# Second norm of a hybrid RWKV-7 / neighbourhood-attention layer: the third token tile finished in two halves, and two low weight halves made by adding DMAs

## The chip, the cores and the metric

The kernel runs on one core of a Trainium2 chip. TensorE (PE) multiplies, VectorE (DVE), ScalarE (ACT) and GpSimd (POOL) do the elementwise work, and SyncE (SP) issues most DMAs. The metric is the device time of one execution in microseconds (us); smaller is better. Before the change three runs gave a median of 1182.05 us (1181.28 to 1182.42).

## The reference, cut to what matters

One layer is applied to 128 context tokens and 512 latent tokens, with D = 1024 features. The change lies in its last third: the second RMS norm and the feed-forward part.

```python
x = x + g1 * (merged @ p["w_out"])
h2 = _rmsnorm(x, p["norm2_g"]) * (1.0 + sc2) + sh2
x = x + g2 * ((jax.nn.silu(h2 @ p["ffn_w1"]) * (h2 @ p["ffn_w3"])) @ p["ffn_w2"])
```

The hidden width of the feed-forward part is 2816, which is 22 tiles of 128 columns. All values are float32.

## The kernel before, in words

**Products.** Every float32 operand x is carried as two rounded tiles, a high half (x cast to fp32r) and a low half (x minus its high half). A product is the sum of three matmuls: high times high, high weight times low activation, low weight times high activation. `mm4` (L1797 to L1806) issues them in that order for four blocks of 128 features, so a group of 12 matmuls reads the weight's low half for the first time at its third matmul. `split` (L188 to L190) makes the two halves of an activation: an ACT cast and a DVE (or POOL) subtraction.

**Tokens.** The 640 tokens are five tiles of 128 (index i, where 0 to 3 are latent, 4 is context). For the feed-forward part they are regrouped into two halves of 320 tokens, n = 0 and n = 1, and the features into two halves q = 0 and q = 1; `hq[q, n]` holds the normed values and `B2[q, n]` their high and low tiles (named b in the trace). Tile 2 is cut in the middle: its first 64 tokens end the half n = 0 and its last 64 begin the half n = 1 (`cuts`, L1744).

**The second norm.** The last matmuls of the output projection (L288, tiles acc and m) are walked by `beside`, a loop that counts them. At given counts, listed in the string `n2`, it issues steps of the norm into the queues of the engines. Per tile i: A adds the projection into x (DVE L1683, L1684), S sums squares (ACT L1721), R takes the reciprocal root (DVE L247, POOL L248), X scales (DVE L1727), T and U transpose the two feature halves on PE (L1734) and apply scale and shift from PSUM (`n_out`: ACT L1740 for two blocks, DVE L1742 for the other two), and H and J split the two feature halves (`n_split`, L189 and L190). W loads and splits a feed-forward weight tile (L167, L177, L179). Steps issued at one count stand in the engines' queues in that order, and each engine works its queue strictly in order.

**After the projection.** The counting loop goes on through the first two hidden tiles (`conv_gen`, PE L1805, tile f), computed as plain products: 24 matmuls for each of two weights, for n = 0 of hidden tiles 0 and 1, then for n = 1. Beside them stand the rest of the norm (tiles 3 and 4), the four Strassen sums of the activations (D, DVE L1764) and their splits (E, tile t), and at count 230 the steps `Y0 Y2 K1 ... K8`: Y is the SiLU and product of a finished hidden tile (`conv_out`, L1823 on), K are the preparations of the first Strassen pair.

**Strassen pairs.** Hidden tiles 2 to 21 are computed by `pair`, one after the other: seven products of 12 matmuls instead of eight. The weights of a pair are g and u, two loaded tiles of 128x1024 (wst), and sums of their halves (ws, L1860, s1 to s4: s3 on POOL, the others on DVE). `preps` gives four weights, a (g itself), b (sums s3 and s1), c and d. Each is split by `w_hl`: the high half is an ACT cast (L1846, whi), the low half a DVE subtraction (L1849, wlo). For the first pair (hidden tile `FA` = 2) K1 to K8 run this in the order "s3 s1 s2 s4 ha la hb lb" (`w0`); for the later pairs the steps are spread over the products of the pair before (`wt`). The first product reads a, the second b, the third a again, and it adds into the sum of the first, which ACT has copied out before (L1886, tile p).

**Buffers.** The tile of g lives in a pool with one buffer, so the load of the next pair's g (SP, L167) waits until the last reader of this pair's g is done.

**The adding DMA elsewhere.** `wcast` (L171 to L180) has a second way to make a low half, used 26 times earlier in the program (between 252 and 601 us): ACT writes the negated rounded value into the low tile (L175), and a DMA issued by POOL adds the unrounded source onto it (L176).

Of the kernel before, what the change touches and what calls it, by code (L numbers as in the profile page):

```python
# [7 lines left out]
F32 = mybir.dt.float32  # L8
F32R = mybir.dt.float32r
AF = mybir.ActivationFunctionType  # L10
ALU = mybir.AluOpType
# [3 lines left out]
P = 128  # L15
# [7 lines left out]
XB, WAB, FA = 4, 8, 2  # L23
# [31 lines left out]
        "2 0 6 6 6 4 4 5 2 0 5 1 1 0 0"),  # L55
    qp=((0, 0, 7, 6, 7), (2, 5, 4, 4, 3, 2, 5, 3, 1)), ada=2, pa=1, pd=0,
    lw=(0, 0, 0, 0, 0, 2, 2, 2, 2, 2, 2, 2, 2, 2, 2, 2),
    n2=("48:A0S0 60:A1S1R0X0 72:A2S2R1X1 74:R2T0 76:U0X2H0J0 86:T1U1H1J1 89:W1 92:W0 100:T2U2H2J2 108:A3S3 "
     "120:A4S4R3X3R4X4W2W3 160:T3U3H3J3 180:T4U4H4J4 200:D1D3D2D4 210:E2E3E1 218:K0E4 "
     "230:Y0Y2K1K2K3K4K5K6K7K8 266:Y1"),  # L60
    te="dddddddd", pf=2, se="pddd", oe="d", w0="s3 s1 s2 s4 ha la hb lb",
# [40 lines left out]
def V(ap, dims, off=0):  # L102

    return bass.AP(ap.tensor, ap.offset + off, [list(ap.ap[0])] + [list(d) for d in dims])
# [3 lines left out]
def body(ctx: ExitStack, tc: tile.TileContext, xs, xp, cols, consts, w_ada, b_row, w_rw, w_qkv,  # L108
# [3 lines left out]
    pe, act, dve, pool, sp = nc.tensor, nc.scalar, nc.vector, nc.gpsimd, nc.sync  # L112

    def open_pool(stack, name, bufs=1, space=None):
        if space is None:
            return stack.enter_context(tc.tile_pool(name=name, bufs=bufs, reuse_waits="tile"))
        return stack.enter_context(tc.tile_pool(name=name, bufs=bufs, reuse_waits="tile", space=space))
# [17 lines left out]
    def nm(s):  # L135
        cn[0] += 1
        return f"{s}_{cn[0]}"
# [19 lines left out]
    def wdma(src, home=None):  # L157
        if len(rot) > 1 and home is None:
            rot.append(rot.pop(0))
        pl, nst, nhl = (rot if home is None else wpool)[-1 if home is None else home] if rot else wpool[-1]  # L160
        st = pl.tile([P, 1024], F32, tag="wst", bufs=nst, name=nm("wst"))
        n = src.shape[1]
        if len(src.shape) == 3:
            sp.dma_start(V(st[:, :], [[src.shape[2], n], [1, src.shape[2]]]), src)
            n *= src.shape[2]
        else:
            sp.dma_start(st[:, :n], src)  # L167
        return st, n, pl, nhl

    def wcast(w, eng=None):  # L170
        st, n, pl, nhl = w  # L171
        hi = pl.tile([P, 1024], F32R, tag="whi", bufs=nhl, name=nm("whi"))
        lo = pl.tile([P, 1024], F32R, tag="wlo", bufs=nhl, name=nm("wlo"))
        if eng is pool:
            act.activation(lo[:, :n], st[:, :n], AF.Copy, scale=-1.0)  # L175
            pool.dma_start(lo[:, :n].bitcast(F32), st[:, :n], accum_op=ALU.add)  # L176
        act.copy(hi[:, :n], st[:, :n])  # L177
        if eng is not pool:
            dve.tensor_tensor(out=lo[:, :n], in0=st[:, :n], in1=hi[:, :n].bitcast(F32), op=ALU.subtract)  # L179
        return hi, lo  # L180

    def wload(src, eng=None):
        return wcast(wdma(src), eng)
# [4 lines left out]
    def split(hi, lo, src, eng=dve):  # L188
        act.copy(hi, src)  # L189
        eng.tensor_tensor(out=lo, in0=src, in1=hi.bitcast(F32), op=ALU.subtract)  # L190
# [54 lines left out]
    def rms_rstd(pl, ssq, n, scale, eps, bufs=2):  # L245
        r = pl.tile([P, n], F32, tag=f"rs{n}", bufs=bufs, name=nm("rs"))
        dve.tensor_scalar(out=r, in0=ssq, scalar1=scale, scalar2=eps, op0=ALU.mult, op1=ALU.add)  # L247
        pool.tensor_tensor(out=r, in0=r, in1=mhalf[:, :n], op=ALU.pow)  # L248
        return r
# [94 lines left out]
    p1 = sb  # L344
# [5 lines left out]
    pp = open_pool(s1a, "pp1a", bufs=2, space=PSUM)  # L350
# [6 lines left out]
    xt, q0 = [], []  # L357
# [14 lines left out]
    def ada_part(k0, n, c0):  # L372

        for kt in range(0, 8, 4 // n):
            w = wa_load(k0, n, kt)
            yield
            for i in range(4 // n):
                ada_mm(psa, w[:, i * 256 * n:(i + 1) * 256 * n], kt + i, 64 * n, c0)
# [40 lines left out]
    with s0:  # L419
        with tc.manual_schedule(engines=START):  # L420
            g = ada_part(0, 2, 0)
# [21 lines left out]
            g = ada_part(2, 2, 128)  # L443
# [7 lines left out]
            g = ada_part(4, 4, 256)  # L451
# [366 lines left out]
    with s1:  # L818
# [25 lines left out]
        with s1a:  # L844
            for b, dst, gcol in ((0, qT, dcol(dqg)), (1, kT, col("kg"))):
# [10 lines left out]
                for i in range(5):  # L856
# [7 lines left out]
                    r = rms_rstd(tb, ssq, 8, 1.0 / 64, 1e-6, bufs=3)  # L864
# [47 lines left out]
        with ExitStack() as s1b:  # L912
            tb = sb = open_pool(s1b, "p1b")
            pp = open_pool(s1b, "pp1b", bufs=2, space=PSUM)
# [157 lines left out]
    with ExitStack() as s3:  # L1072
        sb = open_pool(s3, "p3")
        pp = open_pool(s3, "pp3", bufs=2, space=PSUM)
# [556 lines left out]
    pp = open_pool(ctx, "pp4", bufs=3, space=PSUM)  # L1631
# [37 lines left out]
    G = xpool.tile([P, 2, 1024], F32, name="G")  # L1669
# [10 lines left out]
    def add_gated(ps, i, n, c, a=0, b=512):  # L1680
# [15 lines left out]
                      name=f"b{x[0]}{x[1]}{i}") for i in range(2)] for x in halves2}  # L1696
# [16 lines left out]
    nr = [{} for _ in range(5)]  # L1713
# [13 lines left out]
        dve.tensor_scalar(out=nr[i]["x"], in0=x2[i], scalar1=nr[i]["r"][:, 0:1], scalar2=None, op0=ALU.mult)  # L1727

    def n_out(i, q):
        g = 0 if i < 4 else 1  # L1730
        ps = pp.tile([P, 512], F32, tag="tp", name=nm("xt"))
        for k in range(4):
            kt = 4 * q + k
            pe.transpose(ps[:, k * 128:(k + 1) * 128], nr[i]["x"][:, kt * 128:(kt + 1) * 128], ident)  # L1734
        for n, p0, p1, a in cuts(i):
            for k in range(4):
                kt = 4 * q + k
                src, t = ps[:, k * 128 + p0:k * 128 + p1], hq[q, n][:, k, a:a + p1 - p0]
                if k < 2:
                    act.activation(t, src, AF.Identity, scale=m2[:, kt, g:g + 1], bias=s2[:, kt, g:g + 1])  # L1740
                else:
                    dve.tensor_scalar(out=t, in0=src, scalar1=m2[:, kt, g:g + 1],  # L1742
                                      scalar2=s2[:, kt, g:g + 1], op0=ALU.mult, op1=ALU.add)

    def cuts(i):

        if i == 2:
            return (0, 0, 64, 256), (1, 64, 128, 0)
        return (((0, 0, 128, 128 * i),) if i < 2 else ((1, 0, 128, 128 * i - H2),))

    def n_split(i, q):
        for n, p0, p1, a in cuts(i):
            sl = slice(a, a + p1 - p0)
            split(*[B2[q, n][p_][:, :, sl] for p_ in range(2)], hq[q, n][:, :, sl],
                  pool if PRM["h2e"][2 * i + q] == "p" else dve)
# [14 lines left out]
    def eng_x(c):  # L1770
        return pool if c == "p" else dve

    ffw = {}
    steps = dict(D=t_sum, E=t_split, Y=lambda i: conv_out(i), K=lambda i: first_prep(i), A=n_add, S=n_square, R=n_rstd, X=n_scale, T=lambda i: n_out(i, 0), U=lambda i: n_out(i, 1), H=lambda i: n_split(i, 0), J=lambda i: n_split(i, 1),
                 W=lambda i: ffw.update({i: wload(w13[i])}))
    at, cnt = [(int(n), e) for n, e in (x.split(":") for x in PRM["n2"].split())], [0]

# [42 lines left out]
    def conv_out(i):  # L1820
        ft, n = i // 2, i % 2
        if i not in cps:
            return  # L1823
        if n == 0:
            hidden(ft)
        p1, p3 = cps.pop(i)
        a = sb.tile([P, NT], F32, tag="a", bufs=2, name=nm("a"))[:, :H2]
        act.activation(a, p1[:, :H2], AF.Silu)
        dve.tensor_tensor(out=a, in0=a, in1=p3[:, :H2], op=ALU.mult)
        sl = slice(H2 * n, H2 * n + H2)  # L1830
        split(u[ft][:, 0, sl], u[ft][:, 1, sl], a)


    W = {}

    def w_stage(ft):
        W[ft] = dict(g=wdma(w13[2 * ft], 1), u=wdma(w13[2 * ft + 1], 0))

    def w_hl(w, src, width=1024):

        _, _, pl, nhl = w
        r = []

        def hi():
            r.extend(pl.tile([P, 1024], F32R, tag=t, bufs=nhl, name=nm(t)) for t in ("whi", "wlo"))
            act.copy(r[0][:, :width], src())  # L1846

        def lo():
            dve.tensor_tensor(out=r[1][:, :width], in0=src(), in1=r[0][:, :width].bitcast(F32), op=ALU.subtract)  # L1849
        return hi, lo, r  # L1850

    def w_sum(ft, i):
        w = W[ft]
        a1, a2, b1, b2 = w["g"][0][:, 0:512], w["g"][0][:, 512:1024], w["u"][0][:, 0:512], w["u"][0][:, 512:1024]
# [7 lines left out]
    def preps(ft):  # L1862
        w, r = W[ft], {}
        for k, n, src, wd in (("a", "g", lambda: w["g"][0], 1024), ("b", "u", lambda: w["s"][0], 1024),
                              ("c", "g", lambda: w["s"][1], 1024), ("d", "u", lambda: w["u"][0][:, 512:1024], 512)):
            r["h" + k], r["l" + k], w[k] = w_hl(w[n], src, wd)
        r.update((f"s{i}", lambda i=i: w_sum(ft, i)) for i in (1, 2, 3, 4))
        return r

    def pair(ft, tag, old, now, nxt):  # L1870
# [6 lines left out]
        c2 = sb.tile([P, NT], F32, tag="c2", bufs=1, name=nm("c2"))  # L1877
        w = W[ft]

# [53 lines left out]
    def first_prep(i):  # L1933
        if i == 0:
            w_stage(FA)
            now.update(preps(FA))
        else:
            run(now, PRM["w0"].split()[i - 1])

    fts = [list(range(a, b)) for a, b in zip((0,) + PRM["fp"], PRM["fp"] + (NFT,))]  # L1940
    with tc.manual_schedule(engines=FIRST):
# [144 lines left out]
```

## Time and profile before

| what | us |
|---|---|
| three runs, median (lowest to highest) | 1182.05 (1181.28 to 1182.42) |
| the profiled execution | 1182.22 |
| its span, from the first to the last instruction | 1180.4 |
| outside the span | 1.8 |
| PE busy in the span | 1123.0 |
| DVE busy | 777.8 |
| ACT busy | 531.6 |
| POOL busy | 192.1 |

A timeline row has the start, the duration, the engine, the line, the operation, and what it writes and reads; where the engine sat idle before it, the idle time and what ended it stand in brackets. Rows with "x4" are four instructions in a row. The chain of work that ended last is followed back from the last instruction: it says, at each moment, which work the end was waiting for. PEld is the loading of weights into the array, ahead of the matmul. In the table of stretches of time, PEclk is the granted clock of TensorE as a share of full speed, and the two last columns are the mean busy share of the 16 DMA engines and what they moved.

### The profile page before, as it was taken

How to read it: one execution, taken by the hardware profiler on the slowest of the kernel's cores; microseconds unless marked ns; L12 is line 12 of the kernel's file. 1: busy time of each engine (PE TensorE's matmuls, PEld its weight loads, DVE VectorE, ACT ScalarE, POOL GpSimd, SP SyncE). 2: the span in 40 equal slices, each digit the busy share in tenths (PEclk: the TensorE clock that was granted, in tenths of full speed). 3: DMA queues.
4: the chain of work that ended last, by engine and by line, in shares of the span. 5: the costliest groups of instructions: out<-in, count | busy, mean ns of one | idle time of the engine just before them, and what ended most of it. 6: DMA issues, size and time to landing. Idle time of an engine off the chain costs nothing.

```text
span 1180.4 us, 26871 instructions
## 1 busy us (share of the span) xinstructions
PE 1123.0 (95%) x11160; PEld 995.3 (84%) x11160; DVE 777.8 (66%) x1635; ACT 531.6 (45%) x1050; POOL 192.1 (16%) x260
## 2 busy tenths in 40 slices
PE   6999999899999999999799899999999999999998
PEld 4688877789888988888698777899899989998997
DVE  4565465559558747936486756887568757775775
ACT  4444656554564665556343323554124422441330
POOL 1162244320101202111100141100000000001000
PEclk9999999999999999999899999999999999999999
DMA  9752777654433523433753641312312231232122
GB/s 334 261 116 86 240 224 227 208 137 109 104 83 93 138 69 91 112 102 95 241 151 102 223 161 54 108 54 90 107 54 90 79 101 55 89 107 90 54 79 101
DMA packets 60194, 148.11 MB, mean 125 GB/s; under 512 B 7428, under 2 KB 22404, under 8 KB 60072
## 3 DMA queue, kind: packets, MB, share of 16 engines
q1 hardware_dynamic: 55464, 131.56, 34.1%
q0 software_dynamic: 3744, 13.63, 5.9%
q8 instruction: 88, 1.44, 0.5%
q10 hardware_dynamic: 864, 1.20, 0.3%
q14 instruction: 34, 0.28, 0.1%
HBM read 118.41 MB, written 14.32 MB: 112 GB/s over the span
## 4 chain that ended last, share of the span: by engine, by line
PE 62%; DVE 9%; ACT 3%; issue 3%; DMA 1%; SPq 0%; POOL 0%; DVEq 0%; ACTq 0%; POOLq 0%
PE f L1805 21%; PE acc L288 16%; PE fl L201 12%; PE w L1362 1%; PE w L1389 1%; DVE pr L1288 1%; PE w L1402 1%; DMA o<-o_d 1%; PE w L1374 1%; PE mm L201 1%; PE w L1186 1%; DVE RL L1292 1%; PE w L1380 1%; PE w L1419 1%; PE w L1234 1%
## 5 line engine op out<-in xcount | busy, mean ns | idle before, releaser
L1805 PE MATMUL f<-t,whi 128*128 128x320 f32 x640 | 141.8, 310 | 0.0
L1805 PE MATMUL f<-b,whi 128*128 128x320 f32 x608 | 136.2, 311 | 2.0 <-ACT b L189 1.7
L288 PE MATMUL acc<-whi,u 128*128 128x512 f32 (+1 forms) x448 | 136.0, 385 | 0.0
L201 PE MATMUL fl<-h,whi 128*128 128x320 f32 x672 | 121.2, 320 | 1.3 <-issue 1.3
L177 ACT CAST whi<-wst 128x1024 fp32r<-128x1024 f32 (+1 forms) x77 | 79.2, 1033 | 63.6 <-PE acc L288 43.0
L1805 PEld LDWEIGHTS f<-t,whi 128*128 128x128 f32 x640 | 107.3, 189 | 0.0
L201 PEld LDWEIGHTS fl<-h,whi 128*128 128x128 f32 x672 | 101.4, 188 | 6.1 <-issue 1.4
L1805 PEld LDWEIGHTS f<-b,whi 128*128 128x128 f32 x608 | 102.3, 189 | 3.2 <-ACT b L189 2.1
L1805 PE MATMUL f<-t,wlo 128*128 128x320 f32 x320 | 99.1, 310 | 0.0
L288 PEld LDWEIGHTS acc<-whi,u 128*128 128x128 f32 x448 | 83.5, 188 | 16.6
L1805 PE MATMUL f<-b,wlo 128*128 128x320 f32 x304 | 94.6, 311 | 2.2 <-DVE wlo L1849 2.2
L1846 ACT CAST whi<-ws 128x1024 fp32r<-128x1024 f32 x40 | 42.0, 1051 | 108.7 <-PE f L1805 47.5
L179 DVE TENSOR_TENSOR wlo<-wst,whi 128x1024 fp32r<-128x1024 f32 (+1 forms) x51 | 62.2, 1227 | 38.1 <-ACT whi L177 37.5
L288 PE MATMUL acc<-wlo,u 128*128 128x512 f32 (+1 forms) x224 | 86.3, 385 | 0.0
L1860 POOL TENSOR_TENSOR ws<-wst 128x512 f32<-128x512 f32 x20 | 28.1, 1405 | 340.7 <-DVE wlo L1849 226.7
L288 PE MATMUL acc<-whi,h 128*128 128x512 f32 x240 | 78.1, 399 | 0.9 <-DVE h L413 0.9
L201 PE MATMUL fl<-h,wlo 128*128 128x320 f32 x336 | 63.4, 321 | 0.0
L1683 DVE SCALAR_TENSOR_TENSOR tt<-acc,G 128x512 f32<-128x512 f32 (+1 forms) x51 | 34.5, 679 | 42.8 <-PE acc L288 42.7
L1846 ACT CAST whi<-wst 128x1024 fp32r<-128x1024 f32 (+1 forms) x48 | 41.4, 870 | 42.3 <-PE acc L288 37.6
L1805 PEld LDWEIGHTS f<-t,wlo 128*128 128x128 f32 x320 | 60.2, 188 | 0.0
L1805 PEld LDWEIGHTS f<-b,wlo 128*128 128x128 f32 x304 | 57.5, 189 | 2.5 <-DVE wlo L1849 2.5
L1849 DVE TENSOR_TENSOR wlo<-ws,whi 128x1024 fp32r<-128x1024 f32 x40 | 54.9, 1372 | 6.3 <-ACT whi L1846 6.3
(342 smaller groups left out, 2503.7 us busy)
## 6 DMA issues: line engine op xcount, KB each, us to landing
wst<-in_w_dram SPq DMA_DIRECT2D x66, 512.0 KB
wst<-in_w_rw_dram SPq DMA_DIRECT2D x31, 512.0 KB
wlo<-wst POOLq DMA_DIRECT2D x26, 512.0 KB, 4.6
wa<-in_w_ada_dram SPq DMA_DIRECT2D x24, 512.0 KB
f<-in_w_ada_dram SPq DMA_DIRECT2D x16, 512.0 KB
wst<-in_w_qkv_dram SPq DMA_DIRECT2D x12, 512.0 KB
o<-o_d SPq DMA_DIRECT2D x14, 320.0 KB
x<-in_xs_dram SPq DMA_DIRECT2D x8, 512.0 KB
```

Of the source, the lines that this page charges most:

```text
L177: act.copy(hi[:, :n], st[:, :n])
L179: dve.tensor_tensor(out=lo[:, :n], in0=st[:, :n], in1=hi[:, :n].bitcast(F32), op=ALU.subtract)
L201: pe.matmul(ps[:, :t1 - t0], w[:, a:a + 128], x[:, k0 + kt, t0:t1], start=n == 0, stop=n == 3 * nk - 1)
L288: pe.matmul(pss[i][:, a:b], lhs(x, kt, ts_), w[:, cs_], start=ki == 0 and n == 0, stop=ki == last and n == 2)
L1186: pe.matmul(pr[h][hrows[h ^ i], o_], x[hrows[h], :], R_[hrows[h], l, :], start=True, stop=True)
L1234: pe.matmul(pt[h][hrows[h ^ i], o_], S.BK[l // 10][hrows[h], l % 10, i, :], idh(h), start=True, stop=True)
L1288: dve.tensor_tensor(out=prv, in0=V(RL[:, s + 1 + a, :], [[32, b - a], [0, s]], s), in1=V(RL[:, s, :], [[0, b - a], [1, s]]), op=ALU.mult)
L1683: dve.scalar_tensor_tensor(out=tt, in0=ps[:, a:b], scalar=c, in1=G[:, g, sl], op0=ALU.mult, op1=ALU.mult)
L1805: pe.matmul(ps[:, :H2], w_[:, c_], x_[:, kt, :], start=first and kt + n == 0, stop=last and kt == 3 and n == 2, skip_group_check=more)
L1846: act.copy(r[0][:, :width], src())
L1849: dve.tensor_tensor(out=r[1][:, :width], in0=src(), in1=r[0][:, :width].bitcast(F32), op=ALU.subtract)
L1860: eng_x(PRM["se"][i - 1]).tensor_tensor(out=o_, in0=x, in1=y, op=op)
```

## The change

There are two edits.

**The third token tile in two halves.** `n_out` now applies scale and shift only to the first cut of tile 2, and `n_split` only splits that; a second call (`second=True`, the new steps F and G) applies and splits the other 64 tokens. In the list, the transposes and the first half move from count 100 to count 94, and the second half stands at count 104, still ahead of tile 3's A step at 108.

**Two low halves by adding DMAs.** For the first pair alone, the low halves of the weights a and b are made as `wcast` does it for POOL: ACT negates, a DMA from POOL's queue adds.

```diff
-    n2=("... 92:W0 100:T2U2H2J2 108:A3S3 "
+    n2=("... 92:W0 94:T2U2H2J2 104:F2G2 108:A3S3 "
...
+    def n_mod(i, q, cs_):
+        g, ps = 0 if i < 4 else 1, nr[i][q]
+        for n, p0, p1, a in cs_:
...
-    def n_split(i, q):
-        for n, p0, p1, a in cuts(i):
+    def n_split(i, q, second=False):
+        if second:
+            n_mod(i, q, cuts(i)[1:])
+        for n, p0, p1, a in cuts(i)[1:] if second else cuts(i)[:1]:
...
-    def w_hl(w, src, width=1024):
+    def w_hl(w, src, width=1024, add=False):
...
         def lo():
+            if add:
+                act.activation(r[1][:, :width], src(), AF.Copy, scale=-1.0)
+                pool.dma_start(r[1][:, :width].bitcast(F32), src(), accum_op=ALU.add)
+                return
             dve.tensor_tensor(out=r[1][:, :width], in0=src(), in1=r[0][:, :width].bitcast(F32), op=ALU.subtract)
...
-            r["h" + k], r["l" + k], w[k] = w_hl(w[n], src, wd)
+            r["h" + k], r["l" + k], w[k] = w_hl(w[n], src, wd, ft == FA and k in "ab")
```

How this stands in the queues is shown at three places. On DVE, tile 2 of the norm, between the subtractions of two feed-forward weights and the add of tile 3 (hq are the normed values, 9385 and 9387 of the token half n = 0, 9386 and 9388 of n = 1; b are the low tiles; xt is the PSUM tile):

```order
-L1742 TENSOR_SCALAR hq_9385<-xt_9658,m_9372,s_9373 128x64 x2
-L1742 TENSOR_SCALAR hq_9386<-xt_9658,m_9372,s_9373 128x64 x2
-L1742 TENSOR_SCALAR hq_9387<-xt_9671,m_9372,s_9373 128x64 x2
-L1742 TENSOR_SCALAR hq_9388<-xt_9671,m_9372,s_9373 128x64 x2
+L1745 TENSOR_SCALAR hq_9385<-xt_9652,m_9372,s_9373 128x64 x2
+L1745 TENSOR_SCALAR hq_9387<-xt_9661,m_9372,s_9373 128x64 x2
 L190 TENSOR_TENSOR b_9390<-hq_9385,b_9389 128x4x64
+L190 TENSOR_TENSOR b_9394<-hq_9387,b_9393 128x4x64
+L1745 TENSOR_SCALAR hq_9386<-xt_9652,m_9372,s_9373 128x64 x2
 L190 TENSOR_TENSOR b_9392<-hq_9386,b_9391 128x4x64
-L190 TENSOR_TENSOR b_9394<-hq_9387,b_9393 128x4x64
+L1745 TENSOR_SCALAR hq_9388<-xt_9661,m_9372,s_9373 128x64 x2
```

The two low tiles of n = 0 (9390 and 9394) now come before any work on n = 1; the work on n = 1 follows at once, still ahead of the next step.

On ACT, the end of the plain products and the start of the first pair, before the change:

```order
L1828 ACTIVATE a_9943<-f_9825 128x320
L189 CAST u_9942<-a_9943 128x320
L1846 CAST whi_9954<-wst_9916 128x1024
L1846 CAST whi_9958<-ws_9948 128x1024
L1828 ACTIVATE a_10000<-f_9913 128x320
L189 CAST u_9936<-a_10000 128x320
```

and in the changed kernel at the same place:

```order
L1834 ACTIVATE a_9943<-f_9825 128x320
L189 CAST u_9942<-a_9943 128x320
L1852 CAST whi_9954<-wst_9916 128x1024
L1856 ACTIVATE wlo_9955<-wst_9916 128x1024
L1852 CAST whi_9959<-ws_9948 128x1024
L1856 ACTIVATE wlo_9960<-ws_9948 128x1024
L1834 ACTIVATE a_10002<-f_9913 128x320
```

Two negations of 128x1024 have come into ACT's queue, each behind the cast of its weight; the two subtractions on DVE (L1849, of wlo_9955 and wlo_9959) are gone.

On PE, the first matmuls of the first pair in the changed kernel, with what each waits for (the first product adds up in f_10063, the second in f_10064):

```order
L1811 MATMUL f_10063<-b_9389,whi_9954 128x320 [waits Activation_49]
L1811 MATMUL f_10063<-b_9390,whi_9954 128x320
L1811 MATMUL f_10063<-b_9389,wlo_9955 128x320 [waits DMASW2_49]
L1811 MATMUL f_10063<-b_9389,whi_9954 128x320
L1811 MATMUL f_10063<-b_9390,whi_9954 128x320
```

The order of the matmuls is as before; the third one waited for DVE and now waits for a DMA of POOL's queue (DMASW).

More of the change, by code (lines that the diff above doesn't have):

```diff
@@ L57 @@
     lw=(0, 0, 0, 0, 0, 2, 2, 2, 2, 2, 2, 2, 2, 2, 2, 2),
-    n2=("48:A0S0 60:A1S1R0X0 72:A2S2R1X1 74:R2T0 76:U0X2H0J0 86:T1U1H1J1 89:W1 92:W0 100:T2U2H2J2 108:A3S3 "
+    n2=("48:A0S0 60:A1S1R0X0 72:A2S2R1X1 74:R2T0 76:U0X2H0J0 86:T1U1H1J1 89:W1 92:W0 94:T2U2H2J2 104:F2G2 108:A3S3 "
      "120:A4S4R3X3R4X4W2W3 160:T3U3H3J3 180:T4U4H4J4 200:D1D3D2D4 210:E2E3E1 218:K0E4 "
@@ L1729, in n_out @@
     def n_out(i, q):
-        g = 0 if i < 4 else 1
-        ps = pp.tile([P, 512], F32, tag="tp", name=nm("xt"))
+        ps = nr[i][q] = pp.tile([P, 512], F32, tag="tp", name=nm("xt"))
         for k in range(4):
@@ L1734, in n_out @@
             pe.transpose(ps[:, k * 128:(k + 1) * 128], nr[i]["x"][:, kt * 128:(kt + 1) * 128], ident)
-        for n, p0, p1, a in cuts(i):
+        n_mod(i, q, cuts(i)[:1])
+    def n_mod(i, q, cs_):
+        g, ps = 0 if i < 4 else 1, nr[i][q]
+        for n, p0, p1, a in cs_:
             for k in range(4):
@@ L1749, in cuts @@
         return (((0, 0, 128, 128 * i),) if i < 2 else ((1, 0, 128, 128 * i - H2),))
-    def n_split(i, q):
-        for n, p0, p1, a in cuts(i):
+    def n_split(i, q, second=False):
+        if second:
+            n_mod(i, q, cuts(i)[1:])
+        for n, p0, p1, a in cuts(i)[1:] if second else cuts(i)[:1]:
             sl = slice(a, a + p1 - p0)
@@ L1774, in body @@
     steps = dict(D=t_sum, E=t_split, Y=lambda i: conv_out(i), K=lambda i: first_prep(i), A=n_add, S=n_square, R=n_rstd, X=n_scale, T=lambda i: n_out(i, 0), U=lambda i: n_out(i, 1), H=lambda i: n_split(i, 0), J=lambda i: n_split(i, 1),
+                 F=lambda i: n_split(i, 0, True), G=lambda i: n_split(i, 1, True),
                  W=lambda i: ffw.update({i: wload(w13[i])}))
```

## The prediction

> **What bounds the kernel now.** I read the page first, then the waits of PE behind 740 us, then the chain that ended last, then the timelines of PE, DVE and ACT around the two waits that this shows. The page gives the busy times and the share of the DMA engines in 40 slices of 29.5 us, in tenths; the waits have the time in total, how often, and the longest:
>
> ```profile
> PE 1123.0 (95%) x11160; PEld 995.3 (84%) x11160; DVE 777.8 (66%) x1635; ACT 531.6 (45%) x1050; POOL 192.1 (16%) x260
> DMA  9752777654433523433753641312312231232122
> ...
> PE f L1805 <- DVE wlo L1849: 2.2, 1, 2.2
> PE f L1805 <- ACT b L189: 1.7, 1, 1.7
> PE f L1805 <- DVE b L190: 0.3, 1, 0.3
> ```
>
> PE is the bound, and from the second norm to the end it waits in two places only: 2.0 us before the plain products (for tile b), 2.2 us before the first pair (for wlo). Each is the place of one edit. The chain, in order of time:
>
> ```profile
> 774.36 0.47 ACT u L189
> ...
> 775.26 0.70 DVE ws L1860
> 775.99 0.70 DVE ws L1860
> ...
> 777.32 1.23 DVE wlo L1849
> ...
> 778.59 5.03 PE f L1805 x22
> ...
> 783.65 46.02 PE f L1805 x312
> 829.67 30.40 PE acc L288 x134
> ```
>
> From 778.59 the chain is PE alone, so a microsecond more or less at that point arrives at the end. Before it the chain is ACT and DVE, not PE. That decides the first edit: time that PE wins at 745 us counts only if ACT and DVE also come sooner to 775 us.
>
> **First edit, the third tile.** Rows of PE, then of DVE and ACT:
>
> ```profile
> 743.25 0.39 PE L288 MATMUL acc<-wlo,m 128*128 128x512 f32 x1
> 745.35 0.41 PE L1805 MATMUL f<-b,whi 128*128 128x320 f32 x1 [1.71 <-ACT b L189]
> ...
> 746.27 0.31 PE L1805 MATMUL f<-b,wlo 128*128 128x320 f32 x1
> ...
> 751.84 1.03 PE L1734 MATMUL xt<-K,xn 128*128 128x128 f32 x8
> ...
> 741.73 0.59 DVE L1742 TENSOR_SCALAR hq<-xt,m,s 128x64 f32<-128x64 f32 x2
> 743.08 1.18 DVE L1742 TENSOR_SCALAR hq<-xt,m,s 128x64 f32<-128x64 f32 x4 [0.77 <-ACT hq L1740]
> 745.04 0.59 DVE L1742 TENSOR_SCALAR hq<-xt,m,s 128x64 f32<-128x64 f32 x2 [0.77 <-ACT hq L1740]
> 745.55 1.42 DVE L190 TENSOR_TENSOR b<-hq,b 128x256 fp32r<-128x256 f32 x4
> 746.89 0.68 DVE L1683 SCALAR_TENSOR_TENSOR tt<-acc,G 128x512 f32<-128x512 f32 x1
> 750.34 0.75 DVE L1727 TENSOR_SCALAR xn<-x,rs 128x1024 f32<-128x1024 f32 x1 [0.66 <-POOL rs L248]
> 752.48 2.35 DVE L179 TENSOR_TENSOR wlo<-wst,whi 128x1024 fp32r<-128x1024 f32 x2
> ...
> 740.27 0.69 ACT L1740 ACTIVATE hq<-xt,s,m 128x64 f32<-128x64 f32 x2
> ```
>
> ACT and DVE take turns on the PSUM tile. In the new order ACT does both feature halves of n = 0 without a turn (740.27 to 741.65, twice 0.69), DVE from 741.73 to 742.91 (twice 0.59). A subtraction takes a fourth of 1.42, 0.36, and I take as much for a cast on ACT. The casts follow at 742.36 and 742.95, and the subtractions end at 743.20 and 743.72. PE's last projection matmul starts at 743.25, the next could start at 743.48, and its group reads 9394 only twelve matmuls on. So the whole first wait goes: the third matmul comes at 743.78 (two steps of 0.15) instead of 746.27, a lead of **2.5 us**.
>
> Then the lead is lost. The second half on DVE, counted in the same way: hq_9386 waits for ACT (743.95 to 744.54), ACT casts (to 744.94), DVE subtracts (to 745.36), hq_9388 (745.57 to 746.16), cast (to 746.56), subtraction (746.60 to 746.98). The add of tile 3 starts at 746.9, where it started before: the order has more turns, but work of the other feature half fills them. Everything on DVE behind it stays. PE comes to the transposes of tile 3 at 749.35 and waits there for xn, ready at 750.34 + 0.75 = 751.09: 0.7 us of lead are left. The third matmul of the next group, due at 753.5, waits for wlo, ready at 752.48 + half of 2.35 = 753.7: 0.45 left. At the first pair the high half of a releases PE:
>
> ```profile
> 774.73 1.05 ACT L1846 CAST whi<-wst 128x1024 fp32r<-128x1024 f32 x1
> 776.77 1.04 ACT L1846 CAST whi<-ws 128x1024 fp32r<-128x1024 f32 x1 [0.99 <-DVE ws L1860]
> ...
> 775.88 0.51 PE L1805 MATMUL f<-b,whi 128*128 128x320 f32 x2
> 778.59 0.45 PE L1805 MATMUL f<-b,wlo 128*128 128x320 f32 x1 [2.20 <-DVE wlo L1849]
> ```
>
> It ends at 774.73 + 1.05 = 775.78 either way, and nothing is left. I take **0** for the first edit. Bounds: if both waits of 0.77 went and nothing took their place, the chain would start 1.5 us sooner; if one more turn of 0.77 were added, 0.8 us later.
>
> **Second edit, the adding DMAs.** The trace has the same operation 26 times, as a group of 512 KB issues, and once with all three steps near each other (ACT, then POOL):
>
> ```profile
> wlo<-wst POOLq DMA_DIRECT2D x26, 512.0 KB, 4.6
> DMA to landing us min/median/max: 4.4/4.6/8.9
> L175 ACT ACTIVATE wlo<-wst x26: 1042/1049/1067, 250.8 to 599.2; 128x1024 fp32r<-128x1024 f32 x26
> 599.16 1.06 ACT L175 ACTIVATE wlo<-wst 128x1024 fp32r<-128x1024 f32 x1
> 600.53 0.86 POOL L176 DMA_DIRECT2D wlo<-wst  x1 [6.16 <-ACT wlo L175]
> ```
>
> The new path to the third matmul: the negation follows the cast on ACT at once, from about 775.69 (two in a row overlap by about 0.1, as two subtractions of 1.22 take 2.35) to 776.74. From ACT's end to POOL's issue it takes 600.53 - 600.22 = 0.31, so the issue starts at 777.05. The data is there 4.6 later, at 781.65. DVE's subtraction ended at 777.32 + 1.23 = 778.55. This term is **+3.1 us**; 4.4 gives +2.9, 8.9 gives +7.4. DVE was late because three sums stood ahead of it; the new path passes them, but a wait of 4.6 replaces work of 1.23.
>
> The Trainium skill (page "DMA: Bandwidth & Descriptors", section "Anatomy of one DMA — SWDGE (gpsimd) path") fits a DMA of POOL's queue at about 2.0 us plus the bytes over 436 GB/s, an estimate of 3.2 us for 512 KB; the row above, at least 4.4, disagrees, and the adding form may be why. By that page the term would be +1.7.
>
> The second add: ACT casts 776.77 to 777.81, negates to 778.77, POOL issues at 779.08, it lands at 783.68. PE needs it twelve matmuls after the third. At the slow clock (next paragraph) these take 3.2, so at 784.8: cost **0**, at most 3.2 if it takes 8.9. ACT gets twice 1.05 more work ahead of the SiLUs, DVE loses two subtractions of 1.22; both are off the path here, since the copy L1886 below is needed only 24 matmuls in.
>
> That copy held PE once, because ACT was late with it:
>
> ```profile
> 783.64 0.30 PEld L1805 LDWEIGHTS f<-b,whi 128*128 128x128 f32 x2 [0.28 <-ACT p L1886]
> 778.57 0.33 SPq L167 DMA_DIRECT2D wst<-in_w_dram  x1
> 785.45 0.69 DVE L1860 TENSOR_TENSOR ws<-wst,wst 128x512 f32<-128x512 f32 x1
> ```
>
> With PE 3 us later ACT has it in time: **-0.3**. The load of the next g tile, issued by SP at 778.57 when the subtraction was over, now waits for the first add, so 781.65. Its data is read first at 785.45, off PE's path and for the next pair: 0.
>
> **The clock.** Stretches around the second wait (PE busy and count, PEld, DVE, ACT, POOL, PEclk, DMA share, GB/s):
>
> ```profile
> 774.00:776.20 2.20, 2.20 (x16) 2.08 (x15) 1.58 (x4) 1.41 (x2) 0.00 (x0) 1.00 0.00 0
> 776.20:778.60 2.40, 0.20 (x3) 0.01 (x1) 2.37 (x4) 1.38 (x2) 0.00 (x0) 1.00 0.00 0
> 778.60:782.00 3.40, 3.40 (x13) 3.40 (x14) 2.71 (x4) 0.93 (x3) 1.28 (x1) 0.53 0.49 154
> 782.00:786.00 4.00, 3.98 (x26) 3.71 (x26) 3.19 (x5) 2.35 (x5) 0.00 (x0) 0.97 0.02 4
> ```
>
> After this wait PE ran at clock 0.53 for 3.4 us: 13 matmuls at 0.26 instead of 0.147 each, a loss of 1.5 us. The longer wait pays it too. The Trainium skill ("TensorE: Matmul & The Clock Gate", section "Part 1: The HAM clock gate (the "warmup" mystery)") says that the clock is set in free-running windows of about 3.4 us and comes back after one busy window; the row agrees, and by the page the slow stretch could last up to twice that. By rows alone the extra loss lies between 0 and once more 1.5; I take **+0.2**, near the one stretch that the trace has.
>
> **Sum.** 0 + 3.1 + 0 - 0.3 + 0.2 = +3.0 us on the profiled execution's 1182.22: **1185.2 us**, 0.25% up. The median of the runs lies 0.17 below the profiled one. A measurement of this kernel can tell about 0.2% (2.4 us) from no change, so slower begins at 1184.4. With the landing at 4.4, the clock's 0 to 1.5 and small shifts of the chain this case reaches from 1184.0 to 1186.7.
>
> **Rivals.**
> - *An add lands late.* Two adds and the held load share the DMA engines, and the row's maximum is 8.9: if the second takes that, +3.2 (1188.4); if the first, +4.3 (1189.5). For it: the load now starts inside the second add's transfer. Against: the median sits at 4.6.
> - *An add takes 3.2 us.* It lands at 780.25, 1.4 sooner: 1183.8, no measurable change. The page named above is the reason; the rows speak against.
> - *The chain of ACT and DVE starts sooner* by up to 1.5, if the new turns cost less than I count: 1183.7.
> - *Faster: the add lands almost with its issue.* The DMA engines are idle at 774 to 778.6 (share 0.00), while the 26 were issued between 250 and 601 us, where the page's slices show 2 to 7 tenths. The mechanism decides when a landing takes less than 1.5 us from POOL's start (778.55 - 777.05). At the floor, POOL's 0.86 alone, PE goes on at 777.95: 0.6 sooner, 0.3 for the copy, and a wait of 1.8 like the one at 743 us, which kept its clock: 1.5. Sum -2.4, 1179.8. Against: the minimum of 26 is 4.4.
> - That the change doesn't do what it says, a matmul that waits for something else, is excluded by the order of PE.
>
> **How the numbers follow.** Forecast 0.70, late add 0.13, short add 0.08, earlier chain 0.05, faster 0.04. Slower by over 0.2%: 0.13 and nearly nine tenths of 0.70, 0.73; within 0.2%: 0.23; faster: 0.04. The range goes from 1183.5 to 1188.4: it takes in the short add and the late second one and leaves out the faster case and a late first add.
>
> **What would show it.** In the new trace the wait before the first plain product is gone, a wait of about 1.8 us for xn stands before the transposes of tile 3, and the add of tile 3 starts within 0.3 us of 746.9. The third matmul of the first pair waits about 5.5 us for a DMA, to about 781.7; POOL's issue starts near 777.05 and lands 4.4 to 4.9 later; then PE runs half as fast for 3.4 us or more. I am wrong if the add lands before 780, if the casts of the first pair start over 0.5 us sooner, or if PE waits again for the second add.

## The result and the profile after

The changed kernel takes **1186.19 us** (median of 13 runs, 1184.47 to 1188.92); the kernel before takes 1182.42 (13 runs, 1181.28 to 1186.15). The ratio is 1.003, with a 95% interval of 1.0019 to 1.0041, so it is slower by 2.2 to 4.8 us. The profiled execution took 1185.4 (span 1183.6) against 1182.22 before. The 13 runs spread with their mean granted clock: the seven at 0.986 to 0.988, the profiled one among them, took 1184.47 to 1186.19, and the six at 0.982 to 0.985 took 1186.73 to 1188.92.

PE's waits from the second norm to the end in the changed kernel (total, how often, longest):

```profile
PE f L1811 <- DMA wlo<-wst: 5.2, 1, 5.2
PE xt L1733 <- DVE rs L247: 1.8, 1, 1.8
```

The wait of 2.0 before the plain products is gone, and one of 1.8 stands before the transposes of tile 3. The wait of 2.2 before the first pair has become one of 5.2, and it ends with a DMA. The chain that ended last, from the adding DMA on:

```profile
777.08 4.48 DMA wlo<-wst
781.55 0.04 issue
781.60 51.28 PE f L1811 x334
832.88 40.83 PE acc L288 x180
...
1152.46 27.39 PE acc L288 x132
```

The DMA stands on the chain where DVE stood before, and behind it PE never waits again. The timeline of PE in the changed kernel at the places that the prediction names:

```profile
743.13 0.39 PE L288 MATMUL acc<-wlo,m 128*128 128x512 f32 x1
743.36 0.45 PE L1811 MATMUL f<-b,whi 128*128 128x320 f32 x2
...
751.18 1.09 PE L1733 MATMUL xt<-K,xn 128*128 128x128 f32 x8 [1.79 <-DVE rs L247]
...
775.88 0.56 PE L1811 MATMUL f<-b,whi 128*128 128x320 f32 x2
781.60 0.64 PE L1811 MATMUL f<-b,wlo 128*128 128x320 f32 x1 [5.16 <-DMA wlo<-wst]
...
784.96 0.47 PE L1811 MATMUL f<-t,wlo 128*128 128x320 f32 x1
...
786.96 0.46 PE L1811 MATMUL f<-b,whi 128*128 128x320 f32 x2
```

PE goes on with the first pair at 775.88, as before (775.88), although it had 2 us in hand at 743.36. The work of ACT, DVE and POOL that belongs to it, each from its engine's timeline:

```profile
746.91 0.68 DVE L1683 SCALAR_TENSOR_TENSOR tt<-acc,G 128x512 f32<-128x512 f32 x1
...
774.78 1.05 ACT L1852 CAST whi<-wst 128x1024 fp32r<-128x1024 f32 x1
775.73 1.05 ACT L1856 ACTIVATE wlo<-wst 128x1024 fp32r<-128x1024 f32 x1
...
777.08 0.90 POOL L1857 DMA_DIRECT2D wlo<-wst  x1 [17.78 <-ACT wlo L1856]
779.12 0.87 POOL L1857 DMA_DIRECT2D wlo<-ws  x1 [1.14 <-ACT wlo L1856]
```

Tile 3's add (L1683) starts at 746.91 where it started at 746.89; the cast of the first pair at 774.78 where it started at 774.73. From issue to landing the two adding DMAs took

```profile
DMA to landing us min/median/max: 4.5/5.0/5.4
```

the first 4.5, the second 5.4 (779.12 + 5.4 = 784.5, and PE reads that tile at 784.96).

**A number without the early drift.** From one profile to the next the early program shifts what follows: the last projection matmul starts between 742.45 and 745.92 in the profiles of this study. So for each kernel I also take the **stage**: from the start of the last projection matmul (the row at 743.13 above) to the start of the last block of output matmuls in the chain (1152.46 above). After the change it is 409.33; before it is 1149.25 - 743.25 = 406.00, by this row of the chain before:

```profile
1149.25 27.39 PE acc L288 x132
```

The stage grew by 3.33; the profiled time grew by 3.18, and 743.13 - 743.25 = -0.12 of the difference lies before it.

One sentence ahead of the prediction is wrong: of the four weight sums s1 is on POOL, and s2, s3 and s4 are on DVE; weight b is made of s2 and s3, and c of s1 and s4. Three sums on DVE ahead of the subtraction, which the prediction uses, remain.

### The profile page after: what moved, and what is told of

Same layout as the page of the kernel before. It is cut to its first block, busy times and chain, and to the rows that moved or that the text cites. A ratio compares the mean times of both kernels' runs of the same rounds, so it can differ in the third digit from the quotient of the medians.

```text
span 1183.6 us, 26878 instructions
## 1 busy us (share of the span) xinstructions
PE 1123.9 (95%) x11160; PEld 995.6 (84%) x11160; DVE 776.0 (66%) x1633; ACT 534.0 (45%) x1052; POOL 193.4 (16%) x262
## 4 chain that ended last, share of the span: by engine, by line
PE 62%; DVE 8%; issue 3%; ACT 3%; DMA 2%; SPq 0%; POOL 0%; ACTq 0%; DVEq 0%; POOLq 0%
PE f L1811 21%; PE acc L288 16%; PE fl L201 12%; PE w L1389 1%; PE w L1362 1%; DVE pr L1288 1%; DMA o<-o_d 1%; PE w L1402 1%; PE mm L201 1%; PE w L1374 1%; PE w L1186 1%; DVE RL L1292 1%; PE w L1419 1%; DVE Rt L1322 1%; PE w L1380 1%
## 5 line engine op out<-in xcount | busy, mean ns | idle before, releaser
L1683 DVE SCALAR_TENSOR_TENSOR tt<-acc,G 128x512 f32<-128x512 f32 (+1 forms) x51 | 34.5, 680 | 42.6 <-PE acc L288 42.6
```

The lines of the kernel that those rows point to most:

```text
L1683: dve.scalar_tensor_tensor(out=tt, in0=ps[:, a:b], scalar=c, in1=G[:, g, sl], op0=ALU.mult, op1=ALU.mult)
```

## Experiments

Each was timed in several rounds beside the kernel before (medians 1182.83, 1182.51 and 1182.58 in the three groups: first four rows, next four, last three).

| kernel | median us (range) | ratio to before, 95% interval | stage us |
|---|---|---|---|
| the change | 1186.19 (1184.47-1188.92) | 1.003 (1.0019-1.0041) | 409.33 |
| e1, norm edit alone | 1181.79 (1179.05-1183.6) | 0.9989 (0.9979-0.9999) | 406.15 |
| e2, both adds alone | 1185.0 (1182.53-1188.85) | 1.0019 (1.0006-1.0031) | 408.93 |
| e3, norm edit and a's add | 1186.61 (1183.75-1188.75) | 1.0028 (1.0014-1.0043) | 409.41 |
| e4, the change, clock kept | 1185.4 (1182.46-1187.75) | 1.002 (1.0008-1.0032) | 409.55 |
| e5, norm edit, weights split early | 1180.38 (1177.88-1181.51) | 0.9976 (0.9964-0.9987) | 402.99 |
| e6, before, clock kept | 1182.9 (1181.74-1185.09) | 1.0 (0.9989-1.0012) | 406.05 |
| e7, norm edit and b's add | 1187.52 (1184.33-1192.71) | 1.0043 (1.0028-1.0059) | 410.29 |
| e8, e5 with a's add | 1181.22 (1178.28-1184.71) | 0.9987 (0.9974-1.0001) | 403.56 |
| e9, e5 with the old norm | 1179.37 (1177.93-1181.08) | 0.9974 (0.9962-0.9985) | 402.93 |
| e10, the change, plain DMAs | 1184.73 (1181.15-1187.26) | 1.002 (1.0005-1.0035) | 408.34 |
| e11, the change, adds in halves | 1184.96 (1183.26-1186.51) | 1.0023 (1.0011-1.0036) | 407.58 |

### e1 to e3: one edit at a time

e1, the first edit alone:

```diff
-            r["h" + k], r["l" + k], w[k] = w_hl(w[n], src, wd, ft == FA and k in "ab")
+            r["h" + k], r["l" + k], w[k] = w_hl(w[n], src, wd)
```

> Only the edit of the second norm; the low halves of the first pair stay subtractions on DVE. My theory (the lead of PE at the third tile is given back, because ACT and DVE set when the first pair's high half is ready): no change against the kernel before, within 0.6 us; PE waits about 1.8 us before the transposes of tile 3 in place of the 2.0 us before the plain products, and still 2.2 us for the low half of the first pair. Rival A (the norm's edit wins its 2 us, and the adds cost 5 to 6): 2.0 us faster than before. Rival B (the new order of the norm costs the time, the adds nothing): 3 us slower than before.

e2, the second edit alone, in the kernel before; the norm is untouched:

```diff
-            r["h" + k], r["l" + k], w[k] = w_hl(w[n], src, wd)
+            r["h" + k], r["l" + k], w[k] = w_hl(w[n], src, wd, ft == FA and k in "ab")
```

> Only the adding DMAs, on the norm of before. My theory: as slow as the whole change, 3.0 to 3.8 us above before, with a wait of 5.2 us for the DMA. Rival A: 5 to 6 us above before. Rival B: no change.

e3, the change with the adding DMA for tile a alone:

```diff
-            r["h" + k], r["l" + k], w[k] = w_hl(w[n], src, wd, ft == FA and k in "ab")
+            r["h" + k], r["l" + k], w[k] = w_hl(w[n], src, wd, ft == FA and k == "a")
```

> The whole change, but only the weight a of the first pair by an adding DMA, b by the subtraction on DVE. My theory (the latency of the first add alone counts, the second lands under the first product): as the whole change within 0.6 us, 3.0 to 3.8 us above before. Rival C (two adds that share the engines, and their two negations on ACT, make it slow): half of it or less, at most 1.9 us above before.

PE's waits in the same stretch, of e1:

```profile
PE f L1811 <- DVE wlo L1859: 2.2, 1, 2.2
PE xt L1733 <- DVE rs L247: 1.8, 1, 1.8
```

and of e2:

```profile
PE f L1805 <- DMA wlo<-wst: 5.2, 1, 5.2
PE f L1805 <- ACT b L189: 1.8, 1, 1.8
PE f L1805 <- DVE b L190: 0.3, 1, 0.3
```

The edits hardly touch each other: their stages rise by 0.15 and 2.93, which makes 3.08 of 3.33. The norm edit turns the waits of 1.7 and 0.3 for tile b into one of 1.8 for xn, and its stage is 0.15 above that of before; by the median it may be a little faster, 0.1 to 2.5 us by the interval, which the stage doesn't show. The adds alone raise the stage by 2.93, a's add with the norm edit by 3.41. So the loss is in a's add, and b's add costs nothing behind it. (The first matmul that reads a's low half comes 38.37 to 38.47 after the last projection matmul in e2, e3 and the change, and at 35.34 before.)

### e4 and e6: PE kept busy while it waits

e4 issues 34 more matmuls between PE's second and third matmul of the first product, e6 (on the kernel before) 15; they write a PSUM tile that a later product overwrites.

```diff
-            for _ in mm4(ps, w[k], o_, x_, first=st, more=not st):
-                pass
+            for m_, _ in enumerate(mm4(ps, w[k], o_, x_, first=st, more=not st)):
+                if ft == FA and j == 0 and m_ == 1:
+                    for z in range(34):
+                        pe.matmul(C_, w[k][0][:, 0:128], x_[0][:, 0, :], start=True, stop=True)
```

> The whole change, with 34 more matmuls of 128x320 on PE between the second and the third matmul of the first pair, whose result is overwritten: 34 times 0.147 is 5.0 us, so they fit into the wait of 5.2 us. If the slow clock behind the wait costs what the trace shows (17 matmuls at 0.265 instead of 0.147), this runs 2.0 us faster than the whole change, and more than that against its slower executions, so 1183 to 1184.2 us, with a granted clock of 1.00 throughout. If the clock is not set by PE's idle time, it runs the same as the change, or slower by what the matmuls overrun.

> The kernel before with 15 more matmuls at the place of PE's wait of 2.2 us, into a PSUM tile that is overwritten afterwards, so that PE is busy while it waits and keeps its clock. Theory of the stall-and-clock sum (1.5 us lost to the slow clock, and nothing behind it): 1.5 sooner, 404.5 from the last projection matmul to the last big block. Theory of the second gate: the copy of p on ACT, which PE waited for by 0.28 already, comes no sooner (its place in ACT's order is behind the cast that waits for DVE), so the time won is spent in front of it: 405.7 to 406.0, and a wait of 1.3 to 1.8 for p in the trace.

Stretches of e4 (length, then busy time of PE, PEld, DVE, ACT and POOL, granted clock, DMA share, GB/s):

```profile
776.00:778.00 2.00, 2.00 (x15) 2.00 (x15) 1.26 (x2) 1.97 (x3) 0.90 (x1) 1.00 0.00 0
778.00:781.00 3.00, 3.00 (x23) 3.00 (x21) 1.38 (x3) 1.83 (x5) 0.87 (x1) 1.00 0.91 178
785.00:787.00 2.00, 1.55 (x10) 1.55 (x11) 0.00 (x0) 0.00 (x0) 1.30 (x1) 1.00 0.08 33
```

The clock stays at 1.00, and yet the stage is 409.55. PE's timeline in e4 shows where it went:

```profile
782.05 0.41 PE L1811 MATMUL f<-b,wlo 128*128 128x320 f32 x1 [0.78 <-DMA wlo<-wst]
...
785.45 0.41 PE L1811 MATMUL f<-t,wlo 128*128 128x320 f32 x1 [1.38 <-DMA wlo<-ws]
```

At full clock PE comes to b's low half sooner, and then waits 1.38 for the second add. So the 2.0 that I had expected did not come. But the adds also took longer in this profile, 5.1 and 6.4 in place of 4.5 and 5.4. Had the second taken 5.4, PE would by estimate have gone on at 784.4 (778.97 + 5.4) instead of 785.45, and the stage would be 408.5, 0.8 below the change. By that estimate the second add takes back more than half of the gain; that it takes back all of it is not shown. In e6 PE meets another gate, which its waits show:

```profile
PE f L1805 <- ACT b L189: 1.7, 1, 1.7
PE f L1805 <- ACT p L1886: 1.6, 1, 1.6
PE f L1805 <- DVE b L190: 0.3, 1, 0.3
```

The 1.5 that the clock cost are spent before the third product, waiting 1.6 for the copy of p, which stands in ACT's order behind a cast that waits for DVE. In the kernel before, the time lost to the slow clock is covered: taking it away does not move the end (406.05 and 406.00).

### e7: b's add alone

```diff
-            r["h" + k], r["l" + k], w[k] = w_hl(w[n], src, wd, ft == FA and k in "ab")
+            r["h" + k], r["l" + k], w[k] = w_hl(w[n], src, wd, ft == FA and k == "b")
```

> Both edits, but only tile b's low half by the adding DMA; tile a's by DVE's subtraction. PE then goes on with the first product at 778.5, as before, and wants the low half of b twelve matmuls on, at 781.8 at the slow clock. Theory that the second add was hidden only because the first made PE late: it is issued near 778.1, lands 4.5 to 5.4 later, 782.6 to 783.5, and PE waits 0.8 to 1.7 for it: +0.5 to +1.7 on before. Rival (the second add is free by itself, the whole +3.3 is the first add): no wait for a DMA, 406.0 to 406.2, the time of the first edit alone.

It is the slowest of all, stage 410.29, over 2.5 us more than I expected. PE's timeline:

```profile
778.66 0.41 PE L1811 MATMUL f<-b,wlo 128*128 128x320 f32 x1 [2.21 <-DVE wlo L1859]
...
784.85 0.41 PE L1811 MATMUL f<-t,wlo 128*128 128x320 f32 x1 [2.99 <-DMA wlo<-ws]
```

The add was issued at 779.14, not near 778.1, and took 5.7. Stretches of the same run give the rest:

```profile
779.00:780.00 1.00, 1.00 (x6) 1.00 (x5) 0.49 (x1) 0.45 (x2) 0.86 (x1) 0.57 0.50 82
...
782.00:783.00 1.00, 0.00 (x0) 0.00 (x0) 0.55 (x2) 1.00 (x3) 0.00 (x0) 0.73 1.02 205
783.00:784.00 1.00, 0.00 (x0) 0.00 (x0) 0.79 (x1) 0.38 (x1) 0.00 (x0) 1.00 0.88 168
...
785.00:786.00 1.00, 1.00 (x8) 1.00 (x9) 0.00 (x0) 0.00 (x0) 0.96 (x1) 0.98 0.00 0
...
789.00:790.00 1.00, 1.00 (x7) 1.00 (x6) 0.00 (x0) 0.03 (x1) 0.00 (x0) 0.81 0.68 205
```

Two waits bring two slow stretches. A slice's mean clock gives the moment of the switch, if it only knows 0.5 and 1.0: slow from 779.14 (0.57: 0.14 of the slice at full clock) to 782.54, and from 785.96 to 789.38, 3.4 us each. The clock came back to 1.00 at 783 while PE stood still, and fell again at 786 while PE was busy: that fits a clock that follows what PE did in the stretch before. So the second add is not free by itself. It was hidden in the change because the first add made PE late.

### e5, e8 and e9: the weights split ahead of the SiLUs

e5 has the first edit and both low halves by DVE. The preparations of a and two of the sums come before the first SiLU (steps Y, the finishing of the plain hidden tiles), those of b right behind it, and the other three SiLUs are moved into the pair. C's PSUM tile is taken when its product begins, and the SiLU's tile is in another buffer.

```diff
-      "230:Y0Y2K1K2K3K4K5K6K7K8 266:Y1"),
+      "230:K5K6K1K3Y0K7K4K8K2"),
...
+            if part == 0:
+                old = {k: (lambda i=i: conv_out(i)) for k, i in zip("mio", (2, 1, 3))}
...
-        for i in (0, 2, 1, 3):
-            conv_out(i)
```

e8 is e5 with a's low half by the adding DMA; e9 is the same order on the kernel before, so with the old norm.

> First edit alone, both low halves by DVE, but the weights of the first pair are split ahead of the SiLUs, and conv_out of tiles 2, 1 and 3 comes in the course of the pair. My theory (the chain of ACT and DVE sets the start of the first pair, PE only waits for it): whi of a is ready by about 771.3 and wlo by about 773.6, PE begins the pair when the plain products are done, without a wait and without the slow clock, and the third product is not held by the copy of p. The pair is over about 4 us sooner than before: median near 1178.5, from the last projection matmul to the last big block of the out projection 402 instead of 406.0. Rival (PE is the bound there, and the wait of 2.2 is only moved to the next tile that the SiLUs now deliver later): 406 again, within 0.1% of before.

> As the kernel with the weights split ahead of the SiLUs, but a's low half by the adding DMA. If the cost of the add is its latency less what PE has to do meanwhile, then the same DMA, issued near 772.5 and landing near 777.0, costs PE only 0.5 to 1.3 us where it cost 5.2: 0.5 to 1.5 later than its sister with DVE's subtraction, and still sooner than before. Rival (the add costs through the engines and the DMA traffic that it uses, wherever it stands): 3 us later than its sister, the time of before or worse.

> The weights of the first pair split ahead of the SiLUs, but with the second norm as before the change. It tells what the first edit is worth where the first pair no longer waits for ACT and DVE. My theory (the lead of 2.5 us is spent at the waits for xn and the next wlo, before the first pair): PE waits 2.0 before the plain products again, and from the last projection matmul to the last big block it takes 403.0 to 403.6, at most 0.6 more than its sister with the new norm (402.99). Rival (the lead was only lost at the first pair's high half): the two waits add up, 404.5 to 405.

PE's waits in e5:

```profile
PE xt L1733 <- DVE rs L247: 1.8, 1, 1.8
PE f L1811 <- DVE u L1892: 0.6, 1, 0.6
PE f L1811 <- DVE wlo L1859: 0.4, 1, 0.4
```

and in e9:

```profile
PE f L1805 <- ACT b L189: 1.8, 1, 1.8
PE f L1805 <- DVE u L1882: 0.6, 1, 0.6
PE f L1805 <- DVE b L190: 0.3, 1, 0.3
```

The first pair now starts without a wait for a's low half and with its clock, and the stage is 3.0 below before (I had expected 4: two waits of 0.6 and 0.4 are left). The chain of ACT and DVE ahead of the first pair was the bound, and moving their work, not speeding PE, pays. e5 and e9 differ by 0.06: even here the new norm brings nothing. Its lead ends in the wait of 0.4 for b's low half, which e9 doesn't have. In e8 the add is issued at 771.69:

```profile
771.69 4.45 DMA wlo<-wst
...
776.19 1.75 PE f L1811 x10
```

It takes 4.45 again and PE waits 0.84 for it in place of 5.16; the stage is 0.57 above e5 and 2.44 below before (the median, 1181.22, is not clear of before: its interval ends at 1.0001). So the price is the latency less what PE has to do meanwhile, not the use of the engines.

### e10 and e11: what the add's time is made of

e10 leaves the addition out: the DMAs copy the weights into the low halves, so it doesn't compute the reference's products. Bytes, queue and waits stay.

```diff
-                pool.dma_start(r[1][:, :width].bitcast(F32), src(), accum_op=ALU.add)
+                pool.dma_start(r[1][:, :width].bitcast(F32), src())
```

> The changed kernel with its two adding DMAs made plain copies: the addition is left out, so the low halves hold the weights themselves; bytes, queue, places and waits are the same. If the adding form makes these DMAs slow, they land about 3.2 us after their issue (an estimate by the fit of the Trainium skill's page DMA: Bandwidth & Descriptors, section Anatomy of one DMA, SWDGE path), PE's third matmul comes near 780.3 instead of 781.6, and the stage is 1.3 to 2 shorter than the changed kernel's 409.33. Rival (the time is the queue's and the transfer's, the addition is free): 4.4 to 4.6 and 5.4 as with the addition, 409.3.

Issue to landing of the two DMAs in e10, and one stretch of it (the last two columns are DMA share and GB/s):

```profile
DMA to landing us min/median/max: 2.9/3.0/3.1
```

```profile
779.00:780.00 1.00, 0.00 (x0) 0.00 (x0) 0.08 (x1) 0.89 (x2) 0.14 (x1) 0.87 1.02 422
```

The stretch of the change in which only its adds move:

```profile
780.00:781.00 1.00, 0.00 (x0) 0.00 (x0) 0.81 (x2) 0.49 (x2) 0.00 (x0) 0.50 1.00 197
```

With the DMA engines busy in both, the plain copy moves 422 GB/s and the adding one 197. The adding form is the reason for the 4.5: without it 2.9 to 3.1. The Trainium skill ("DMA: Bandwidth & Descriptors", section "Anatomy of one DMA — SWDGE (gpsimd) path") gives about 2.0 us plus the bytes over 436 GB/s, by estimate 3.2 here. The plain copy comes near that (2.9 to 3.1), the adding one does not (4.5). PE's third matmul came 1.55 sooner than in the change (36.92 after the last projection matmul, not 38.47), but the stage is only 1.0 shorter: from its third matmul PE ran at half speed for 5.8 us (780.81 to 786.6), in the change for 4.5 (781.60 to 786.1). The slice of e10 in which its clock came back:

```profile
786.00:787.00 1.00, 1.00 (x6) 1.00 (x6) 0.00 (x1) 0.00 (x0) 0.00 (x0) 0.72 0.09 16
```

e11 splits each add into two of 256 KB:

```diff
-                pool.dma_start(r[1][:, :width].bitcast(F32), src(), accum_op=ALU.add)
+                for z in (0, width // 2):
+                    pool.dma_start(r[1][:, z:z + width // 2].bitcast(F32), src()[:, z:z + width // 2], accum_op=ALU.add)
```

> The changed kernel with each adding DMA split in two of 128x512 (256 KB), the half that PE reads first ahead. If most of the 4.5 us depend on the bytes, the first half lands 2.6 to 3.2 after its issue, PE's wait falls from 5.2 to 3.3-4, and the stage comes to 407.5 to 408.3; the second half, issued 0.9 later, is there before the third product. Rival (most of it is a fixed time of the queue): 4 or more for the first half too, and the stage stays within 0.5 of 409.3, or gets longer since POOL has four issues of 0.9 in a row.

Issue to landing over the four, the weight load (PEld) of PE's third matmul and that matmul, and the slice in which the clock came back:

```profile
DMA to landing us min/median/max: 3.3/4.1/5.2
```

```profile
781.76 0.29 PEld L1811 LDWEIGHTS f<-b,wlo 128*128 128x128 f32 x1 [4.29 <-ACT u L189]
781.79 0.60 PE L1811 MATMUL f<-b,wlo 128*128 128x320 f32 x1 [4.06 <-ACT a L1834]
```

```profile
784.00:785.00 1.00, 1.00 (x5) 1.00 (x5) 1.00 (x1) 0.17 (x1) 0.00 (x0) 0.56 1.18 203
```

The bracket of the matmul names an ACT instruction that ends at the same moment (781.35 + 0.43), but the weight load had started before that end. It fits the first half's landing: POOL's issue starts at 778.38, the shortest landing is 3.3 later, at 781.7, and in the change too the weight load follows the landing by 0.04. Half the bytes save 1.1 of 4.5. By the rates above, 0.524 MB take 2.66 us in the adding form and 1.24 as a copy, and the difference of 1.4 is about that of the first landings (4.5 and 2.9); the remaining 1.7 to 1.8 is nearly the same in both. Halving 2.66 would save 1.3, a little more than was measured. The stage fell by 1.75: 1.1 from the landing, the rest from a shorter slow stretch (half speed ended at 784.9). It is still slower than before.

## Why the prediction came out as it did

The forecast was 1185.2, with slower by over 0.2% as the likeliest; the median is 1186.19 and the profiled execution, against which the sum was made, 1185.4. By its own terms, each measured as a part of the stage:

| term | predicted | measured | from |
|---|---|---|---|
| first edit | 0 | +0.17 | cast of whi 31.65 after the last projection matmul, before 31.48 |
| first add | +3.1 | +2.96 | from that cast to the third matmul 6.82, before 3.86 |
| second add | 0 | 0 | no wait; it landed 0.4 ahead of its reader |
| copy of p | -0.3 | -0.28 | the wait of 0.28 is gone |
| clock | +0.2 | +0.6 | see below |
| rest of the stage | 0 | -0.1 | third product to last block 365.50, before 365.60 |
| sum | +3.0 | +3.3 | stage 409.33 and 406.00 |

- **First edit.** Right, place by place: the wait went, 1.79 for xn came, tile 3's add stayed (746.91), and the pair's cast stayed. e1 and e9 show that it is worth nothing with either start of the pair. That the chain of ACT and DVE was the reason is shown by e5, which moved it.
- **First add.** Right: issue at 777.08 (predicted 777.05), landing 4.48 later (predicted 4.6). The alternative of 3.2 was a copy's time; e10 shows that the adding form makes the difference, as the prediction supposed.
- **Second add.** Right in the result, but with some luck, by a margin of 0.4 where the prediction had 1.1: it took 5.4 rather than 4.6, and the slow clock, which gave it time, lasted longer. e4 and e7 show the cost that it has when PE is on time.
- **The clock** is the term that was mis-sized. From the third matmul to the first of the third product PE took 786.96 - 781.60 = 5.36; before it was 783.65 - 778.59 = 5.06 with the wait of 0.28 for p in it. So the slow clock cost 0.58 more, where 0.2 was taken out of 0 to 1.5: behind the third matmul it lasted 4.5 us, before 3.4. The stretches of the change:

```profile
779.00:780.00 1.00, 0.00 (x0) 0.00 (x0) 0.49 (x1) 0.44 (x2) 0.87 (x1) 0.65 1.00 201
...
786.00:787.00 1.00, 1.00 (x8) 1.00 (x8) 0.00 (x0) 0.00 (x0) 0.05 (x1) 0.94 0.09 16
```

By the slices' means it was slow from 779.30 to 786.12, 6.8 us or two stretches of 3.4, of which PE was waiting until 781.60. The prediction read the 3.4 of before as what follows a wait; but here the slow stretch began at 779.30, 2.9 us after PE stopped at 776.44 and 2.3 before it went on, so a longer wait lies partly inside it. The Trainium skill ("TensorE: Matmul & The Clock Gate", section "Part 1: The HAM clock gate (the "warmup" mystery)") has free-running windows of about 3.4 us; at least one idle window brings the slow clock, and at least one busy window the full one. The 3.4, 3.4 and 6.8 of e7 and of the change agree with such windows. That a whole window must be idle is not what the runs show: waits of 2.2 (before, e1 and e7) were enough. How much of the slow time falls into the wait depends on where the two meet: a wait of 3.63 in e10 brought two stretches (0.87 at 779, back at 786.56), one of 4.06 in e11 a single one (from 781.46, where the slice has 0.73, to 784.88). So the rows of before could bound this term but not size it. That the sum still came within 0.2 of the profiled time is in part luck: +0.38 here and +0.17 in the first edit stand against small misses the other way.
- **The rivals.** The faster one needed a landing in under 1.5; whole adds took 4.4 to 6.4 in these profiles, and the shortest were those that began with the DMA engines idle. A late second add did not happen in the change, though it stood 0.4 away. The earlier chain is excluded by 774.78.

What stays open: the median is 0.8 above the profiled execution, and the runs spread over 4.5 us along with their mean clock; what sets that clock from run to run is not known. Why the adds took longer in e4 (5.1 and 6.4) than in the change is not shown either. In e4 one packet of instruction loading (0.02 MB) ran among them, between 781.4 and 781.6 and with 30.6% of the 16 DMA engines' time there, about 1 us of one engine; the change has none at that place.

## What to carry to other kernels

Where one engine's order of work sets the start of a stage, a cheaper instruction elsewhere buys nothing, and a DMA in place of a late subtraction costs its whole latency: issue it that much ahead of its reader (e8, which is still no faster than e5), or bring the subtraction itself forward (e5 and e9, the only versions here that are clearly faster than before, 0.9976 and 0.9974). Before taking a wait away, look for the gates right behind it: the copy of p took back all that a kept clock had won, and the second add more than half by estimate.

## What the runs showed of the hardware

- A POOL DMA of 512 KB within SBUF that adds moved 197 GB/s with all 16 DMA engines busy and landed 4.4 to 4.5 us after its issue when it was the first (5.1 in e4), and 5.2 to 6.4 after it when another add or a load was under way already. The same DMA as a plain copy moved 422 GB/s and landed after 2.9 to 3.1.
- The clock of PE changed in stretches of 3.4 us. It fell to half 2.2 to 4.1 us after PE had stopped (2.2 in e2, 776.54 to 778.76; 2.7 and 4.1 in e7, 776.45 to 779.14 and 781.86 to 785.96), in e7 with PE busy again by then, and came back while PE stood still (e7, 782.5). After the waits of 1.7 to 1.8 in the second norm it never fell in these profiles; after 2.2 it did in all three that have such a wait (before, e1 and e7). A longer wait need not bring more: 3.63 in e10 brought 6.8 us of half clock, 4.06 in e11 3.4.
